# The first and the last stretch of a two-layer hybrid encoder: zeros ahead of the data, squares in place, later tables, a shorter last root, outputs on two queues

## The chip, the core and the metric

The kernel runs on one core of a Trainium2 chip. The metric is the device time of one execution in microseconds. The core's engines work from queues of their own, each in order: TensorE (PE, with its weight loads as PEld), VectorE (DVE), ScalarE (ACT), GpSimd (POOL) and SyncE (SP), which issues the DMAs.

## What is computed

Two layers, each with four sequence mixers behind one input projection, a cross attention and an MLP; a norm at the end. x is 512 rows of 1024, all in float32.

```python
for l in range(DEPTH):
    h = rmsnorm(x, norm_mix[l])
    z = h @ w_in[l]
    (rq, rk, rv, rg, lx, lg, cq, ckv, kr, gqkv, gg, gb, ga) = split_cols(z, IN_SIZES)
    y_a = retention(rq, rk, rv, rg, positions, ret_gn[l])
    y_b = rg_lru_branch(lx, lg, ...)
    y_c = mla(cq, ckv, kr, positions, ...)
    y_d = gated_deltanet(gqkv, gg, gb, ga, ...)
    x = x + jnp.concatenate([y_a, y_b, y_c, y_d], axis=-1) @ w_out[l]
    x = x + memory_xattn(rmsnorm(x, norm_xattn[l]), rmsnorm(mem, norm_mem[l]), ...)
    h = rmsnorm(x, norm_mlp[l])
    x = x + jnp.square(jax.nn.relu(h @ mlp_w1[l])) @ mlp_w2[l]
return rmsnorm(x, final_norm)
```

rmsnorm divides each row by the root of its mean square; retention and mla turn their queries and keys by tables of cosines and sines of the positions (the tables).

## The kernel before

x lies in SBUF with its 1024 features on the partitions: eight tiles `xr[k]` of 128x512. A float32 product is made of three matmuls at a reduced-precision type: both operands are split into a high part (an ACT copy, `xh`, `wh`) and a low part (a DVE subtraction, `xl`, `wl`), and hi x hi, lo x hi and hi x lo are summed in PSUM (`mm3_cm`, L287). A plain f32 matmul is recorded as two instructions.

**Weights** come in units of 128x1024 (some of 128x720), in the order of `PLAN`. `wload` (L262) issues one unit's DMA on SP, splits it on ACT and DVE; there are two raw buffers, three of `wh`, two of `wl`. `wnext` (L279) keeps two units loaded ahead.

**Order of the work.** The program is traced in Python order, and a planner orders each engine's queue ahead of time by priority and by when it reckons an instruction to be ready. `lane(key, base)` (L201) gives the instructions traced in it a priority: within a layer the weights (w) come first, then evacuations (ev, 1.5), LRU (1.7), gated DeltaNet (gdn, 2), MLA (3), retention (4) and the projections themselves (proj, 6). What is traced outside a lane, at the start of the program, comes ahead of all of these. On the chip each queue runs in that fixed order.

**The start.** L408 to L419 issue the DMAs of the parameters and of x, with the first three weight units among them, the constants and the positions. `norm_tile` (L372) then scales and splits each x tile and squares it on ACT (`square_acc`, L364): the first square is the accumulator `acc` (`xg[2]`), the others go through one buffer `sq` and are added by POOL, the last by DVE. `rope_tables` (L424), called at L1393 ahead of the layers, makes `cosT` and `sinT` with some 26 DVE instructions on 128x128 in one chain and two sines on ACT.

**The gdn projection.** In `layer` (L466), `rstd_of(acc)` (L383) sums the squares over partitions with the ones product (`acc` x `ones`, four f32 matmuls), takes the mean and its inverse root with `rsqrt` (L336: an integer guess and three Newton steps, 12 DVE instructions). It is traced in the gdn lane ahead of `proj_g("gdn", ...)` (L512), whose four units of 24 matmuls write four PSUM banks (two pj, two ch). `bcast` (L393) spreads the inverse root by four matmuls against the identity and an ACT copy. Then six blocks each go through `evz` (a product with the broadcast, L516), a causal convolution (`conv_in`, L521: one ACT and three DVE instructions), tanh, and the gate product `s2[i]` on DVE (L544), beside the projections that follow. The LRU's constants (L914 to L923) are a softplus on 128x2 and a few more tiny DVE steps in the LRU lane, and the DMA of its weights.

**The end.** `last_tile` (L1211) works the last block of the MLP's second product in two halves of 256 columns: a half's products (`prod`), their evacuation and squares (`evac`), the root by `rstd_of(accs[g], 2)`, and `finish(g)`: the broadcast, eight products of 128x256 with it (five on DVE, three on POOL) and eight output DMAs, all issued by SP (L1242).

Of the kernel before, what the change touches and what calls it, by code (L numbers as in the profile page):

```python
# [165 lines left out]
def build(tc, A, out, dbg=None):  # L166
# [63 lines left out]
    def act(o, i, f, **k):  # L230
        ACT.activation(o, i, f, **k)  # L231
# [30 lines left out]
    def wload():  # L262
        u = wstate["loaded"]
        if u >= total:
            return
        wstate["loaded"] += 1
        l, i = divmod(u, len(PLAN))
        n = PLAN[i][1]
        off = l * LAYER_ELEMS + UOFF[i]
        with using("w"):  # L270
            raw = wp.tile([128, n], F32, tag="wraw", name=nm("wr"), bufs=2)
            SP.dma_start(out=raw, in_=A["wu"][off:off + 128 * n].rearrange("(p n) -> p n", p=128))
            hi = wp.tile([128, n], F32R, tag="whi", name=nm("wh"), bufs=3)
            act(hi, raw, AF.Copy)
            lo = wp.tile([128, n], F32R, tag="wlo", name=nm("wl"), bufs=2)
            tt(V, lo, raw, hi.bitcast(F32), SU)
        wstate["tiles"][u] = (hi, lo)

    def wnext(name):  # L279
# [40 lines left out]
    def proj_t(name, xh, xl, n, kper, outs, share=1, ks=None, edge=(True, True)):  # L320
# [12 lines left out]
                        mm(o, xl[k][:, s], wh[:, c], False, edge[1] and k == e1 and t % share == share - 1)  # L333
        return outs

    def rsqrt(o, v, n):  # L336
        t = tiny.tile([128, n], I32, tag=f"rt{n}", name=nm("rt"))
        w = tiny.tile([128, n], F32, tag=f"rw{n}", name=nm("rw"))
        nv = tiny.tile([128, n], F32, tag=f"rn{n}", name=nm("rn"))
        ts(V, t, v.bitcast(I32), 1, ALU.logical_shift_right)  # L340
        ts(V, o.bitcast(I32), t, -1.0, MU, float(0x5f3759df), AD)
        ts(V, nv, v, -0.5, MU)
        for _ in range(3):
            tt(V, w, o, o, MU)
            tt(V, w, w, nv, MU)
            stt(o, w, 1.5, o, AD, MU)
# [33 lines left out]
        acc = xp.tile([128, S], F32, tag="acc", name=nm("acc"))  # L380
        return xh, xl, acc

    def rstd_of(acc, ntt=TT):  # L383
        ps = sct()
        for t in range(ntt):
            mm(ps[:, t:t + 1], acc[:, t * 128:(t + 1) * 128], ones, True, True)
        v = tiny.tile([128, ntt], F32, tag=f"rv{ntt}", name=nm("rv"))
        ts(V, v, ps[:, 0:ntt], 1.0 / D, MU, EPS, AD)
        r = tiny.tile([128, ntt], F32, tag=f"rstd{ntt}", name=nm("rstd"))
        rsqrt(r, v, ntt)  # L390
        return r

    def bcast(r, n=S, pool=None, keep=False):  # L393
# [20 lines left out]
    for l in range(1, NL):  # L414
        SP.dma_start(out=par[l], in_=A["par"][l])
    xg = new_xg()
    for k in range(KT):
        norm_tile(xr[k], P(0, "nmix", k), xg[0][k], xg[1][k], xg[2], k)
    SP.dma_start(out=posi, in_=A["pos"])  # L419

    cosT = cp.tile([128, TT, 32], F32, name="cosT")
    sinT = cp.tile([128, TT, 32], F32, name="sinT")
# [43 lines left out]
    def layer(l):  # L466
# [38 lines left out]
            a, b = pjt(), pjt()  # L505
            return [p[:, i * n:(i + 1) * n] for p in (a, b) for i in range(2)]

        with lane(*GDN):
            rstd = rstd_of(acc)
            rstdh = o16("rstdh", 4)  # L510
            ts(V, rstdh, rstd, 0.5, MU)
        pg = proj_g("gdn", xh, xl, [pjt, pjt, cht, cht])  # L512
        with lane(*GDN):
            rbc = bcast(rstd)

# [20 lines left out]
        for i in range(6):  # L536
            ps = pg[i] if i < 4 else proj_m("gdn", i - 4, xh, xl, new=pjt)
            with lane(*GDN):
                ca = g2()
                zq.append(evz(ps, xtmp(i)))  # L540
                conv_in(zq[i], "gcw", i * 4, ca)
                th = g2()
                act(th, ca, AF.Tanh, scale=0.5)
                stt(s2[i], th, 1.0, ca, AD, MU)  # L544
                if i < 4:
                    act(zq[i], s2[i], AF.Square)
        with lane(*GDN):
            for i in range(4):
                for t in range(TT):
                    mm(ssq[:, t * 8 + 2 * i:t * 8 + 2 * i + 2], zq[i][:, t * 128:(t + 1) * 128], C("hsel"), True, True)  # L550
# [360 lines left out]
        with lane(*MLA):  # L911
            mla()

        with lane(*LRU):  # L914
            spl, sp2, spn, sp4 = o16("spl", 2), o16("sp2", 2), o16("spn", 2), o16("bah", 4)
            ts(V, spl, P(l, "lam", 0, 2), -1.0, MU)
            softplus(sp2, spl, 2)
            ts(V, spn, sp2, -4.0, MU)
            ts(V, sp2, sp2, 2.0, MU)
            ts(V, sp4[:, 0:2], P(l, "lba", 0, 2), 0.5, MU)  # L920
            ts(V, sp4[:, 2:4], P(l, "lbx", 0, 2), 0.5, MU)
            wl_ = op.tile([128, 4, 128], F32, tag="wlru", name=nm("wlru"))
            SP.dma_start(out=wl_, in_=A["wlru"][l])  # L923
# [287 lines left out]
        def last_tile(facc, hh, hl, r2):  # L1211
# [22 lines left out]
            def finish(g):  # L1234
                s = slice(g * 256, g * 256 + 256)
                b, bp = bcast(rs[g], 256, mp, True)
                for m in range(8):
                    if m in (2, 5, 7):
                        tt(G, xr[m][:, s], xr[m][:, s], b, MU)
                    else:  # L1240
                        tt(V, xr[m][:, s], xr[m][:, s], bp, MU)
                    SP.dma_start(out=out[:, m, s], in_=xr[m][:, s])  # L1242

            prod(0, range(16))
            evac(0)
            prod(1, range(8))
            rs[0] = rstd_of(accs[0], 2)
            prod(1, range(8, 16))
            evac(1)
            finish(0)  # L1250
            rs[1] = rstd_of(accs[1], 2)
            finish(1)

        pv = [[bank("lg"), cht()], []]
# [135 lines left out]
            xg = nx  # L1390
        stk.close()

    rope_tables()  # L1393
    for l in range(NL):
        layer(l)
    ctx.close()
# [79 lines left out]
```

## Time and profile before

| | us |
|---|---|
| median of the runs | 1670.68 |
| the runs | 1667.58, 1674.56, 1670.68 |
| span of the profiled execution, first to last instruction | 1662.2 |
| TensorE busy | 1629.5 |
| VectorE busy | 909.0 |
| ScalarE busy | 679.0 |
| GpSimd busy | 105.9 |

The profile is that of one execution; the page gives its span and no other time of it. Times in the rows are microseconds from the span's start. An engine counts as busy from the start of an instruction to its modelled end, so matmuls that follow one another overlap, and their spacing is read from the starts. PEclk is the TensorE clock that was granted, as a share of 2.4 GHz.

### The profile page before, as it was taken

What the parts mean: (1) busy time and instruction counts of PE and PEld (TensorE: products, weight loads), DVE (VectorE), ACT (ScalarE), POOL (GpSimd) and SP (SyncE); (2) the same over time, 40 slices, a digit from 0 to 9 for tenths busy, and PEclk for the clock granted to TensorE, in tenths of its full rate; (3) what the DMA queues carried; (4) which work ended last, traced back from release to release, by engine and by line L of the source; (5) the groups of instructions that cost most, each with busy time, mean ns of one, the idle gap of its engine ahead of it and who ended that gap; (6) DMA issues with size and microseconds to landing.
All of it is one profiled execution on the core that took longest, in us unless ns stands there. A gap on an engine that the chain in (4) does not pass through costs nothing.

```text
span 1662.2 us, 23657 instructions
## 1 busy us (share of the span) xinstructions
PE 1629.5 (98%) x9408; PEld 1343.6 (81%) x9408; DVE 909.0 (55%) x1989; ACT 679.0 (41%) x1169; POOL 105.9 (6%) x96
## 2 busy tenths in 40 slices
PE   6999999999999999999999999999999999999997
PEld 5868789888888888888886787998888888888886
DVE  6886578455555422443368855774563643234433
ACT  5565454344443312432235545543453432124331
POOL 2000000110010010000101000002001000100011
PEclk8999999999999999999999999999999999999998
DMA  4211023332122222223331111253312222222222
GB/s 169 84 39 52 27 92 124 138 122 81 51 90 97 93 97 94 101 90 120 114 103 58 52 40 38 87 168 133 106 52 76 93 98 99 92 99 92 101 89 77
DMA packets 47919, 150.69 MB, mean 91 GB/s; under 512 B 5696, under 2 KB 9792, under 8 KB 47808
## 3 DMA queue, kind: packets, MB, share of 16 engines
q1 hardware_dynamic: 47808, 149.17, 26.3%
q8 instruction: 74, 1.21, 0.3%
q14 instruction: 37, 0.30, 0.1%
HBM read 144.96 MB, written 4.19 MB: 90 GB/s over the span
## 4 chain that ended last, share of the span: by engine, by line
PE 90%; DVE 5%; DMA 2%; ACT 1%; issue 1%; POOL 0%; SPq 0%; POOLq 0%; ACTq 0%; DVEq 0%
PE pj L234 28%; PE ch L234 28%; PE gd L234 23%; PE lg L234 8%; DMA wr<-in_wu 2%; PE ch L402 2%; DVE wl L219 1%; ACT wh L231 1%; DMA mem<-in_memT 1%; DVE g L649 1%; DVE bf L228 0%; DVE sp L222 0%; DVE xl L222 0%; POOL x L219 0%; DVE kv L219 0%
## 5 line engine op out<-in xcount | busy, mean ns | idle before, releaser
L219 DVE TENSOR_TENSOR wl<-wr,wh 128x1024 fp32r<-128x1024 f32 (+1 forms) x256 | 311.3, 1216 | 553.3 <-PE pj L234 181.0
L231 ACT ACTIVATE wh<-wr 128x1024 fp32r<-128x1024 f32 (+1 forms) x256 | 269.6, 1053 | 622.1 <-PE pj L234 204.6
L234 PE MATMUL pj<-xh,wh 128*128 128x512 f32 x288 | 115.6, 402 | 6.8 <-ACT wh L231 6.8
L234 PE MATMUL pj<-xl,wh 128*128 128x512 f32 x288 | 115.6, 401 | 0.0
L234 PE MATMUL pj<-xh,wl 128*128 128x512 f32 x288 | 114.8, 399 | 0.0
L219 POOL TENSOR_TENSOR acc<-acc,sq 128x512 f32<-128x512 f32 x42 | 64.6, 1537 | 762.4 <-ACT sq L231 762.4
L234 PE MATMUL pj<-wh,xl 128*128 128x256 f32 (+1 forms) x352 | 107.5, 306 | 0.0
L234 PE MATMUL ch<-xh,wh 128*128 128x512 f32 x272 | 106.9, 393 | 0.0
L234 PE MATMUL ch<-xl,wh 128*128 128x512 f32 x272 | 106.6, 392 | 0.0
L234 PE MATMUL ch<-xh,wl 128*128 128x512 f32 x272 | 106.4, 391 | 0.0
L234 PE MATMUL pj<-wh,xh 128*128 128x256 f32 (+1 forms) x352 | 106.3, 302 | 0.0
L234 PE MATMUL pj<-wl,xh 128*128 128x256 f32 (+1 forms) x352 | 105.3, 299 | 0.0
L234 PE MATMUL ch<-hh,wh 128*128 128x512 f32 x192 | 75.8, 395 | 0.0
L234 PE MATMUL ch<-hl,wh 128*128 128x512 f32 x192 | 75.8, 395 | 0.0
L234 PE MATMUL ch<-hh,wl 128*128 128x512 f32 x192 | 75.8, 395 | 0.0
L234 PEld LDWEIGHTS pj<-wh,xl 128*128 128x128 f32 x352 | 68.5, 194 | 4.0 <-issue 1.8
L234 PEld LDWEIGHTS pj<-wh,xh 128*128 128x128 f32 x352 | 68.3, 194 | 3.2 <-issue 0.9
L234 PEld LDWEIGHTS pj<-xh,wh 128*128 128x128 f32 x288 | 55.0, 191 | 19.3 <-ACT wh L231 6.8
L234 PEld LDWEIGHTS pj<-wl,xh 128*128 128x128 f32 x352 | 68.4, 194 | 2.4 <-issue 0.8
L219 DVE TENSOR_TENSOR hl<-s,hh 128x512 fp32r<-128x512 f32 x64 | 44.2, 691 | 39.2 <-ACT hh L231 39.0
L234 PEld LDWEIGHTS pj<-xl,wh 128*128 128x128 f32 x288 | 54.8, 190 | 13.2 <-issue 2.3
L234 PEld LDWEIGHTS pj<-xh,wl 128*128 128x128 f32 x288 | 54.7, 190 | 12.6 <-issue 0.9
(533 smaller groups left out, 3791.0 us busy)
## 6 DMA issues: line engine op xcount, KB each, us to landing
wr<-in_wu SPq DMA_DIRECT2D x248, 512.0 KB, 3.5
x<-in_xT SPq DMA_DIRECT2D x16, 256.0 KB, 3.7
wr<-in_wu SPq DMA_DIRECT2D x8, 360.0 KB, 2.8
mem<-in_memT SPq DMA_DIRECT2D x16, 128.0 KB, 3.4
xs<-x SPq DMA_DIRECT2D x8, 256.0 KB, 2.6
x<-xs SPq DMA_DIRECT2D x8, 256.0 KB, 3.2
out<-x SPq DMA_DIRECT2D x16, 128.0 KB, 1.8
big<-in_wmla SPq DMA_DIRECT2D x2, 640.0 KB, 5.9
```

The costliest lines, as they stand in the source:

```text
L219: e.tensor_tensor(o, a, b, op=op)
L231: ACT.activation(o, i, f, **k)
L234: PE.matmul(o, lhsT=l, rhs=r, start=st, stop=sp, **k)
L402: PE.transpose(o, i, ident)
L649: V.transpose(Nt3[32 * q:32 * q + 32].rearrange("m j i -> m i j"), src)
```

## The change

Ten places, all in the first stretch and the last, but for the LRU constants, which are moved in both layers.

- `wload`: the first unit is loaded and split in two column halves, each with its own DMA, ACT copy and DVE subtraction.
- The start: `acc` is first set to zero on DVE, and three f32 matmuls on it (512, 512 and 256 columns) are issued on TensorE into the bank lg. The x tiles are scaled and split without the squares.
- `first_acc`: the squares are made later, on ACT, in place over the x tiles (the first into `acc`), and added by DVE. It is traced ahead of the gdn projection's third unit, in the proj lane (layer 0).
- `norm_in`: the ones product and the root are traced ahead of the fourth unit in the proj lane (layer 0), or as before ahead of the first in the gdn lane (layer 1).
- `rope_tables` is traced behind the fourth gate product, outside any lane; `tc.issue_after(after.ins)` puts those of its instructions that run on DVE behind that product in DVE's queue (an order of issue, no wait). The LRU constants' DVE instructions get the same bound, in both layers.
- `rsqrt1` takes the place of `rsqrt` in `last_tile`: a root on ACT, a reciprocal and one Newton step on DVE.
- The outputs of odd m are issued by ACT, the others by SP.

```diff
@@ -269,11 +269,15 @@
         off = l * LAYER_ELEMS + UOFF[i]
         with using("w"):
             raw = wp.tile([128, n], F32, tag="wraw", name=nm("wr"), bufs=2)
-            SP.dma_start(out=raw, in_=A["wu"][off:off + 128 * n].rearrange("(p n) -> p n", p=128))
+            src = A["wu"][off:off + 128 * n].rearrange("(p n) -> p n", p=128)
             hi = wp.tile([128, n], F32R, tag="whi", name=nm("wh"), bufs=3)
-            act(hi, raw, AF.Copy)
             lo = wp.tile([128, n], F32R, tag="wlo", name=nm("wl"), bufs=2)
-            tt(V, lo, raw, hi.bitcast(F32), SU)
+            cuts = [slice(0, n // 2), slice(n // 2, n)] if u == 0 else [slice(0, n)]
+            for c in cuts:
+                SP.dma_start(out=raw[:, c], in_=src[:, c])
+            for c in cuts:
+                act(hi[:, c], raw[:, c], AF.Copy)
+                tt(V, lo[:, c], raw[:, c], hi[:, c].bitcast(F32), SU)
         wstate["tiles"][u] = (hi, lo)
 
     def wnext(name):
@@ -333,6 +337,16 @@
                         mm(o, xl[k][:, s], wh[:, c], False, edge[1] and k == e1 and t % share == share - 1)
         return outs
 
+    def rsqrt1(o, v, n):
+        w = tiny.tile([128, n], F32, tag=f"rw{n}", name=nm("rw"))
+        nv = tiny.tile([128, n], F32, tag=f"rn{n}", name=nm("rn"))
+        act(o, v, AF.Sqrt)
+        ts(V, nv, v, -0.5, MU)
+        V.reciprocal(o, o)
+        tt(V, w, o, o, MU)
+        tt(V, w, w, nv, MU)
+        stt(o, w, 1.5, o, AD, MU)
+
     def rsqrt(o, v, n):
         t = tiny.tile([128, n], I32, tag=f"rt{n}", name=nm("rt"))
         w = tiny.tile([128, n], F32, tag=f"rw{n}", name=nm("rw"))
@@ -380,14 +394,14 @@
         acc = xp.tile([128, S], F32, tag="acc", name=nm("acc"))
         return xh, xl, acc
 
-    def rstd_of(acc, ntt=TT):
+    def rstd_of(acc, ntt=TT, root=rsqrt):
         ps = sct()
         for t in range(ntt):
             mm(ps[:, t:t + 1], acc[:, t * 128:(t + 1) * 128], ones, True, True)
         v = tiny.tile([128, ntt], F32, tag=f"rv{ntt}", name=nm("rv"))
         ts(V, v, ps[:, 0:ntt], 1.0 / D, MU, EPS, AD)
         r = tiny.tile([128, ntt], F32, tag=f"rstd{ntt}", name=nm("rstd"))
-        rsqrt(r, v, ntt)
+        root(r, v, ntt)
         return r
 
     def bcast(r, n=S, pool=None, keep=False):
@@ -414,9 +428,22 @@
     for l in range(1, NL):
         SP.dma_start(out=par[l], in_=A["par"][l])
     xg = new_xg()
+    warm = xg[2]
+    V.memset(warm, 0.0)
+    wps = bank("lg")
+    for n in (512, 512, 256):
+        mm(wps[:, 0:n], warm[:, 0:128], warm[:, 0:n], True, True)
     for k in range(KT):
-        norm_tile(xr[k], P(0, "nmix", k), xg[0][k], xg[1][k], xg[2], k)
+        gc = P(0, "nmix", k)
+        act(xg[0][k], xr[k], AF.Copy, scale=gc)
+        stt(xg[1][k], xr[k], gc, xg[0][k].bitcast(F32), MU, SU)
     SP.dma_start(out=posi, in_=A["pos"])
+
+    def first_acc():
+        for k in range(KT):
+            act(xr[k] if k else xg[2], xr[k], AF.Square)
+            if k:
+                tt(V, xg[2], xg[2], xr[k], AD)
 
     cosT = cp.tile([128, TT, 32], F32, name="cosT")
     sinT = cp.tile([128, TT, 32], F32, name="sinT")
@@ -505,11 +532,20 @@
             a, b = pjt(), pjt()
             return [p[:, i * n:(i + 1) * n] for p in (a, b) for i in range(2)]
 
-        with lane(*GDN):
-            rstd = rstd_of(acc)
-            rstdh = o16("rstdh", 4)
-            ts(V, rstdh, rstd, 0.5, MU)
-        pg = proj_g("gdn", xh, xl, [pjt, pjt, cht, cht])
+        rs_ = {}
+
+        def norm_in(u):
+            if l == 0 and u == 2:
+                with using("proj"):
+                    first_acc()
+            if u == (3 if l == 0 else 0):
+                with (using("proj") if l == 0 else lane(*GDN)):
+                    rs_["r"] = rstd_of(acc)
+                    rs_["h"] = o16("rstdh", 4)
+                    ts(V, rs_["h"], rs_["r"], 0.5, MU)
+
+        pg = proj_g("gdn", xh, xl, [pjt, pjt, cht, cht], pre=norm_in)
+        rstd, rstdh = rs_["r"], rs_["h"]
         with lane(*GDN):
             rbc = bcast(rstd)
 
@@ -541,9 +577,14 @@
                 conv_in(zq[i], "gcw", i * 4, ca)
                 th = g2()
                 act(th, ca, AF.Tanh, scale=0.5)
-                stt(s2[i], th, 1.0, ca, AD, MU)
+                last = V.scalar_tensor_tensor(s2[i], th, 1.0, ca, op0=AD, op1=MU)
                 if i < 4:
                     act(zq[i], s2[i], AF.Square)
+            if i == 3:
+                after = last
+                if l == 0:
+                    with tc.issue_after(after.ins):
+                        rope_tables()
         with lane(*GDN):
             for i in range(4):
                 for t in range(TT):
@@ -911,7 +952,7 @@
         with lane(*MLA):
             mla()
 
-        with lane(*LRU):
+        with lane(*LRU), tc.issue_after(after.ins):
             spl, sp2, spn, sp4 = o16("spl", 2), o16("sp2", 2), o16("spn", 2), o16("bah", 4)
             ts(V, spl, P(l, "lam", 0, 2), -1.0, MU)
             softplus(sp2, spl, 2)
@@ -1239,16 +1280,16 @@
                         tt(G, xr[m][:, s], xr[m][:, s], b, MU)
                     else:
                         tt(V, xr[m][:, s], xr[m][:, s], bp, MU)
-                    SP.dma_start(out=out[:, m, s], in_=xr[m][:, s])
+                    (ACT if m % 2 else SP).dma_start(out=out[:, m, s], in_=xr[m][:, s])
 
             prod(0, range(16))
             evac(0)
             prod(1, range(8))
-            rs[0] = rstd_of(accs[0], 2)
+            rs[0] = rstd_of(accs[0], 2, rsqrt1)
             prod(1, range(8, 16))
             evac(1)
             finish(0)
-            rs[1] = rstd_of(accs[1], 2)
+            rs[1] = rstd_of(accs[1], 2, rsqrt1)
             finish(1)
 
         pv = [[bank("lg"), cht()], []]
@@ -1390,7 +1431,6 @@
             xg = nx
         stk.close()
 
-    rope_tables()
     for l in range(NL):
         layer(l)
     ctx.close()
```

## Rows read from the trace of the kernel before

**Rows 1.** The page, part 1: busy time and share of each engine.

```profile
PE 1629.5 (98%) x9408; PEld 1343.6 (81%) x9408; DVE 909.0 (55%) x1989; ACT 679.0 (41%) x1169; POOL 105.9 (6%) x96
```

**Rows 2.** Waits of PE over the whole span: us in total, times, longest.

```profile
PE pj L234 <- ACT wh L231: 6.8, 1, 6.8
...
PE gd L234 <- DVE acc L219: 6.4, 1, 6.4
...
PE gd L402 <- DVE kv L219: 1.0, 1, 1.0
```

**Rows 3.** Timeline, end of the span: start, us, engine, line, op.

```profile
1650.97 0.15 DVE L228 TENSOR_SCALAR rv<-gd 128x2 f32<-128x2 f32 x1
...
1653.16 0.16 DVE L222 SCALAR_TENSOR_TENSOR rstd<-rw,rstd 128x2 f32<-128x2 f32 x1
...
1653.46 1.20 PE L234 MATMUL gd<-cst,rstd 128*128 128x128 f32 x4 [2.75 <-DVE rstd L222]
...
1655.97 3.76 SPq L1242 DMA_DIRECT2D out<-x  x8
```

**Rows 4.** Busy time by stretch, columns first; layer 0, then layer 1.

```profile
core 0: us, PE busy (x) PEld busy (x) DVE busy (x) ACT busy (x) POOL busy (x), PEclk, DMA share, GB/s
6.84:42.54 35.70, 29.26 (x113) 23.40 (x113) 28.52 (x75) 18.39 (x27) 9.55 (x6) 0.86 0.44 159
42.54:326.65 284.11, 281.65 (x2298) 232.53 (x2297) 203.31 (x584) 143.78 (x306) 8.36 (x12) 0.99 0.24 79
...
830.15:854.34 24.19, 24.11 (x114) 19.65 (x112) 13.99 (x47) 7.16 (x11) 0.00 (x0) 1.00 0.36 129
854.34:1143.73 289.39, 285.13 (x2298) 235.37 (x2297) 205.37 (x584) 144.73 (x306) 8.50 (x12) 0.98 0.24 78
```

**Rows 5.** Timeline of PE, first 43 us.

```profile
9.97 0.63 PE L234 MATMUL pj<-xh,wh 128*128 128x512 f32 x1
...
10.40 0.63 PE L234 MATMUL pj<-xl,wh 128*128 128x512 f32 x1
...
25.35 1.86 PE L234 MATMUL gd<-cst,acc 128*128 128x1 f32 x8 [6.40 <-DVE acc L219]
...
37.09 0.40 PE L234 MATMUL pj<-xh,wh 128*128 128x512 f32 x1
```

**Rows 6.** Groups of instructions, first 61 us: busy, mean ns | idle.

```profile
L219 POOL TENSOR_TENSOR acc<-acc,sq 128x512 f32<-128x512 f32 x6 | 9.5, 1591 | 11.5 <-ACT sq L231 11.5
```

**Rows 7.** Timeline of all engines, first 45 us.

```profile
2.81 0.20 ACT L231 ACTIVATE sp<-spl 128x2 f32<-128x2 f32 x1 [0.79 <-DVE spl L226]
...
5.14 0.61 ACT L231 ACTIVATE acc<-x 128x512 f32<-128x512 f32 x1
...
5.73 1.06 ACT L231 ACTIVATE wh<-wr 128x1024 fp32r<-128x1024 f32 x1
...
6.95 0.72 ACT L231 ACTIVATE xh<-x,par 128x512 fp32r<-128x512 f32 x1 [0.16 <-DMA x<-in_xT]
...
8.44 0.91 SPq L410 DMA_DIRECT2D x<-in_xT  x2
...
30.67 1.28 ACT L231 ACT_TABLE_LOAD   x1
```

**Rows 8.** Timeline of DVE, 20 to 63 us.

```profile
23.70 0.16 DVE L428 CAST pf<-posi 128x4 f32<-128x4 int32 x1
...
38.43 0.22 DVE L228 TENSOR_SCALAR cosT<-rn__186 128x128 f32<-128x128 f32 x1
...
61.88 0.69 DVE L222 SCALAR_TENSOR_TENSOR g<-g,g 128x512 f32<-128x512 f32 x1 [0.62 <-ACT g L231]
```

**Rows 9.** Timeline of PE, 80 to 84 us.

```profile
82.23 1.98 PE L234 MATMUL gd<-g,cst 128*128 128x512 f32 x4
```

**Rows 10.** DMA, first 16 us (us to landing), then rates of 1655.9 to 1661.2.

```profile
x<-in_xT SPq DMA_DIRECT2D x8, 256.0 KB, 5.9
...
GB/s 0 0 0 0 0 0 54 309 340 248 170 340 325 186 232 363 302 132 278 340 278 124 348 317 240 193 340 348 132 255 356 302 124 309 356 255 23 0 0 0
```

## The prediction, made before the change was run

> **What bounds the kernel now.** I read the busy shares first. TensorE is busy for 1629.5 of 1662.2 us [rows 1], so there are 32.7 us of idle time in the whole span, and only what lies in idle time or at the low clock can be won. The waits of TensorE, longest first, say where: 6.8 us before the first matmul and 6.4 us at the ones product that sums the squares [rows 2]; every wait inside the two layers is 1.0 us or less. The rest of the large idle time lies at the end, where the last matmuls, those of a broadcast, start only at 1653.46 [rows 3].
>
> The third view cuts layer 0 and layer 1 at the same points of their work: from the first matmul of the gdn projection to the first matmul of its next part (96 matmuls of 128x512, the ones product, the broadcast), and from there to the last product of w_out with the same tile [rows 4]. Layer 0 takes 35.70 and 284.11 us, layer 1 takes 24.19 and 289.39 us. The same work costs layer 0 11.5 us more at its start: that is what the change can win there. But the rest costs layer 1 5.3 us more: it idles for 4.3 us against 2.5, and its mean clock is 0.98 against 0.99. A layer that starts without a stall gave part of it back.
>
> In the front itself [rows 5] the matmuls begin at 6.84, are 0.43 us apart (9.97 to 10.40; 512 columns at 1.2 GHz), and 0.227 us apart later (24 of them from 37.09 to 42.54, the cut of [rows 4]: 2.4 GHz). The ones product starts at 25.35 after 6.40 us of idle time. The granted clock of the stretch is 0.86 [rows 4], since it fell to half in that idle time. Stretches before 11.3 us show a clock of 1.00 although the matmuls are 0.43 us apart, so there I go by the spacing.
>
> Why the ones product is late is read on ACT and POOL. POOL adds six squares at 1.59 us each and waits 11.5 us for them [rows 6]. ACT's next square has one buffer and so waits for POOL, and the splits of x and of the weights queue behind it on ACT.
>
> **The change, part by part.** Times are on the profiled execution's clock.
>
> *First matmul.* The square that ran from 5.14 to 5.73 goes [rows 7]. The weight split follows at 5.14 on half the columns; 0.61 us (the square's duration for 512 columns) instead of 1.06. With the 0.05 us hand-over of now (5.73 + 1.06 to 6.84) the first matmul starts at 5.80; I take 5.85. This needs the first half of the weights by 5.14; all of them were there by 5.73, so the bounds are 5.80 and 6.40. The extra DMA on SP costs SP one issue, beside transfers that are still under way.
>
> *Matmuls on zeros.* They wait for a memset of 512 columns on DVE, between 0 and the 0.69 us of a step of two inputs of that size [rows 8]: ready by about 1.5. Two f32 matmuls of 512 columns, recorded as four instructions, take 1.98 us at full clock [rows 9], so 0.43 each with the drain of the last one taken off; the zeros (512, 512 and 256 columns) are worth five of them, at half clock 4.3 us, done by 5.8. So they end just as the first true matmul may start: cost 0, and at most 0.3. What they should buy is the full clock from the first true matmul.
>
> *Unit 0.* The second x tile lands at 6.95 [rows 7]; its split takes ACT and DVE some 0.7 each, until 8.4, and with two more matmuls the seventh may start at 8.85 (now 9.97). So six matmuls spread over 3.0 us where 1.36 would do: 1.64 us that stay lost. The rest of the front at full clock is what layer 1 takes: 5.85 + 1.64 + 24.19 = 31.7, against 42.54. That is 10.8 us. If the clock were half until 11.25 as now, five or six matmuls cost 0.2 us more each: 1.1 us less won.
>
> *Squares in place, ones product later.* ACT's squares (eight, 0.61 each) leave the front of its queue, POOL's six adds leave POOL, and DVE gets six more, 0.69 each as its other steps of two inputs and 512 columns [rows 8]. Each in-place square now also waits until DVE has split its x tile. ACT can't split the last x tile before it lands: issued by 9.35 [rows 7], 5.9 us to landing [rows 10], so near 15.3 and, with its split, 16.0. The eight squares and one weight split after it are at most 5.9 us more, about 21.9; the last add follows at 22.6. The ones product now stands after three units: 5.85 + 1.64 + 72 x 0.227 = 23.8. So it is covered by 1.2 us. If the cover is gone, TensorE waits again; bounds 0 to 2.5 us, I take 0.5. Behind it on TensorE stands unit 3. What is late next is the broadcast, which needs the root; its steps are no longer mixed with the tables on DVE, and unit 3 (5.45 us) covers it.
>
> *Tables and LRU constants.* On DVE the tables run from 23.70 to 38.65, 15 us with other work between [rows 8]; the LRU constants are 20 tiny steps at 0.16 [rows 3], 3.2 us. Both go behind the fourth gdn gate product (now at 61.88 [rows 8], then some ten us sooner). The issue order is bound on DVE only: the LRU weights' DMA on SP isn't moved, and nothing new waits on SP. The two sine activations on ACT follow by their data, with two table loads as now (1.28 each [rows 7]). What queues behind them are the last two gdn convolutions and the weight splits of the moment. DVE and ACT aren't the bound there while TensorE has projections to do, so I cost it at nothing by itself and put it into the term below. In layer 1 the constants move too: 3.2 us on DVE, 0 for the time, bounds plus and minus 1.
>
> *Given back in the mixer.* Between 0 (layer 0's rest as it is) and 5.3 us (layer 1's rest) [rows 4]. Layer 1 is the nearer row for a start without a stall, yet about 3 us of the 5.3 are clock (2% of 289 less 1% of 284), and nothing in these rows ties that to the start. I take the middle, 2.6.
>
> *Last root.* Now 12 DVE steps after the sum: from 1650.97 to 1653.32 [rows 3]. Then: the sum's step, one ACT root (0.20, [rows 7]), four DVE steps at 0.20 apart, two hand-overs: 1.2 us, so 1.1 are saved. The root's table load lies in ACT's idle time. But ACT now issues outputs too, and the root may stand behind one or two of them at 0.48 each: I take off 0.4 and count 0.7, bounds 0.1 and 1.1. The broadcast after it takes 1.20 at half clock, and may come before the clock falls: 0 to 0.6, I take 0.3.
>
> *Outputs by two queues.* Eight issues run from 1655.97 for 3.76 us [rows 3], 0.48 apart. Halved, that would save 1.9 us. But the row of rates [rows 10] shows 340 to 363 GB/s in its best slices: 131 kB in 0.37 us, so the transfers themselves allow only 7 x 0.11 = 0.8, and some tenths more for an earlier first issue. I take 1.0, bounds 0.5 and 1.9. The Trainium skill, "DMA: Bandwidth & Descriptors", section "Issuing engines are not separate DMA queues", speaks against more: several issuing engines share the same transfer engines and save only issue time. By that rule alone the term is 0.8; by the issue pace alone it would be 1.9.
>
> **Sum.** Front 10.8 - 0.5, mixer -2.6, end 0.7 + 0.3 + 1.0: 9.7 us. The span would go from 1662.2 to 1652.5. The median of the runs is 1670.68, 8.5 us above this span, with runs from 1667.58 to 1674.56; the same 9.7 us off it gives 1661.0.
>
> **The rivals.**
> A, the forecast: TensorE stays the bound and at most 4 us come back. For it: waits of TensorE inside the layers are tiny in both layers [rows 2, 4]. With none given back 1658.4; with 4 given back, 1662.4.
> B, all of layer 1's loss appears, or a little more, since the tables add to DVE in a stretch where it is already busy: 10.3 - 5.3 + 2.0 = 7.0 us, 1663.7. For it: layer 1 itself. Against: most of the loss is clock.
> C, the change doesn't do what it says: the squares come late, because ACT does them last and each waits for DVE, and TensorE waits at the ones product as before, at half clock after it. 6 of the 10.8 us go: 1667.0.
> D, slower: the tables set the time. If the gdn chain on DVE, not TensorE, decides the end of the mixer, then 15 + 3.2 us of steps and 2.6 us of table loads stand in it after the fourth gate product, and the chain starts only the front's 10.3 us sooner: 10.5 us late, less 2.0 at the end: 1679.2. It decides from the point at which TensorE runs out of projections. Against it: TensorE's idle time from 42.54 on is 2.5 us in 284 [rows 4].
>
> **How the numbers follow.** A 0.60, B 0.26, C 0.10, D 0.04. The time is A's, 1661.0. A measurement of this kernel can tell about 0.5%, 8.4 us, from no change: faster means below 1662.3. That is A; B and C are within; D is slower: 0.60, 0.36, 0.04. The range of 8 in 10 reaches from A's best case (10.8 at the front, nothing given back, 3.6 at the end: 1656.3, less 2 for the runs' spread) to C: 1654.5 to 1667.5.
>
> **What would show it.** First true matmul near 5.9 and matmuls 0.227 apart from about 9; no TensorE wait at the ones product, now behind 72 matmuls; the first matmul of the next part near 32; the same last product of w_out in layer 0 near 319, not 326.65; root to broadcast 1 us shorter; eight last outputs in about 3 us on two queues. It is wrong if TensorE shows new waits of over 2 us between 40 and 330 (for weight splits held behind the tables on DVE or the sine on ACT), or if the ones product still waits.

## The result, and the profile after

The changed kernel is slower: 1679.91 us in the median (1674.06 to 1686.86) against 1672.15 us of the kernel before beside it, a ratio of 1.0069 [1.0044, 1.0093]. The forecast was 1661.0, faster. The profiled execution of the changed kernel took 1682.89 us, its span is 1681.1 us. Executions of one kernel differ by how long TensorE's clock is at half in each, so the tables below give the span times its mean granted clock (what it would be at full clock) beside the time. The medians leave out the runs more than 1.5% above the fastest of their kernel (one each of e1, e6 and e7, two each of e2 and e8, three of e14, which lost 42 to 67 us to the clock); the profiles of e7 and e14 are of such runs and are read for the order of the work and its waits.

The span splits at the same points of the work as [rows 4], in us:

| stretch | before | after | forecast |
|---|---|---|---|
| start to the first matmul of the next part | 42.54 | 31.46 | 32.2 |
| from there to the same last product of w_out | 284.11 | 314.90 | 286.7 |
| to the ones product of the last half (at 1650.11, 1669.91) | 1323.46 | 1323.55 | as before |
| from there to the end | 12.09 | 11.19 | 10.1 |

The front gave 11.1 us (10.3 forecast); the end gave 0.9 of 2.0; all the rest is one number, 30.8 us lost in the mixer of layer 0 between these two profiles. Busy time by stretch of the kernel after, for the first two lines (us; busy time and count of each engine; PEclk is the granted clock as a share of 2.4 GHz):

```profile
core 0: us, PE busy (x) PEld busy (x) DVE busy (x) ACT busy (x) POOL busy (x), PEclk, DMA share, GB/s
5.84:31.46 25.62, 24.71 (x114) 19.61 (x113) 18.91 (x38) 15.74 (x23) 0.00 (x0) 1.00 0.67 232
31.46:346.36 314.90, 311.55 (x2298) 256.16 (x2297) 210.42 (x634) 147.67 (x313) 8.00 (x12) 0.88 0.22 72
```

The second line has the same 2298 matmuls as [rows 4] and no more idle time than before to speak of (3.4 us against 2.5), but a mean clock of 0.88 against 0.99. TensorE's waits in that stretch of the kernel after (total, times, longest) show that nothing holds it up:

```profile
engine line waited for: us in total, times, longest us
PE lg L234 <- DVE xt L222: 1.0, 1, 1.0
PE ch L416 <- DVE qf L219: 0.8, 1, 0.8
PE gd L234 <- DVE g L717: 0.5, 1, 0.5
PE ch L416 <- ACT o L231: 0.4, 1, 0.4
PE ch L416 <- DVE bf L219: 0.2, 1, 0.2
```

So the place is looked for by the clock, in slices of 20 us. The kernel after, and then the kernel before:

```profile
140.00:160.00 20.00, 20.00 (x256) 17.33 (x251) 4.86 (x16) 4.77 (x14) 0.00 (x0) 0.50 0.08 28
160.00:180.00 20.00, 20.00 (x140) 16.03 (x138) 4.79 (x18) 7.25 (x21) 0.00 (x0) 0.50 0.00 1
180.00:200.00 20.00, 20.00 (x97) 14.19 (x95) 8.07 (x29) 4.76 (x14) 0.00 (x0) 0.50 0.09 27
200.00:220.00 20.00, 20.00 (x118) 15.02 (x118) 7.45 (x29) 5.52 (x15) 0.00 (x0) 0.65 0.01 1
```

```profile
140.00:160.00 20.00, 20.00 (x253) 17.22 (x250) 11.63 (x23) 11.62 (x25) 0.00 (x0) 0.91 0.13 41
160.00:180.00 20.00, 20.00 (x177) 15.55 (x175) 12.30 (x42) 8.06 (x22) 0.00 (x0) 1.00 0.19 66
180.00:200.00 20.00, 20.00 (x173) 15.74 (x173) 11.36 (x42) 9.67 (x28) 0.00 (x0) 1.00 0.08 28
```

TensorE is at 1.2 GHz for 60 us, for 14 of the next 20 (0.65) and for the last one before 140, some 75 us; in the kernel before for 3.6 us. It shows as busy all the time (its last wait before that, 0.5 us, ended at 135.7), and DVE is busy for 4.8 us of 20 where it was for 11.6: nobody waits for DVE. Half of 75 is 37 us (1.8 in the kernel before); 30.8 us more than before show in the stretch.

What TensorE does there is the gated DeltaNet's triangular solve (matmuls of 16 and 32 columns) and then its scan. The groups of matmuls from the solve's first to the scan's first product, in the kernel after (143.3 to 164.7):

```profile
L234 PE MATMUL gd<-g,g 32*32 32x32 f32 x128 | 7.3, 237 | 0.0
L234 PE MATMUL gd<-g,g 16*32 16x16 f32 x128 | 6.4, 210 | 0.0
L234 PE MATMUL pj<-wh,xh 128*128 128x256 f32 x5 | 2.6, 520 | 0.0
L234 PE MATMUL pj<-wl,xh 128*128 128x256 f32 x5 | 2.2, 449 | 0.0
L234 PE MATMUL pj<-wh,xl 128*128 128x256 f32 x5 | 2.1, 415 | 0.0
```

and in the kernel before (136.8 to 157.0):

```profile
L234 PE MATMUL pj<-wh,xl 128*128 128x256 f32 x21 | 6.9, 326 | 0.0
L234 PE MATMUL pj<-wh,xh 128*128 128x256 f32 x21 | 6.6, 314 | 0.0
L234 PE MATMUL pj<-wl,xh 128*128 128x256 f32 x21 | 6.2, 295 | 0.0
L234 PE MATMUL gd<-g,g 32*32 32x32 f32 x128 | 4.8, 192 | 0.0
L234 PE MATMUL gd<-g,g 16*32 16x16 f32 x128 | 3.9, 178 | 0.0
```

The small matmuls are the same; beside them stood 63 wide ones of the projections and now 15. Ahead of the solve the trace counts 489 wide matmuls instead of 368: TensorE came early, the solve came late (143.3 instead of 136.8), and the projections were used up in between. That is what I set out to test; a count beside a clock is no cause yet.

### The profile page after: what moved, and what is told of

Its sections match the earlier page's. It is cut to its first block, busy times and chain, and to the rows that moved or that the text cites. A ratio compares the mean times of both kernels' runs of the same rounds, so it can differ in the third digit from the quotient of the medians.

```text
span 1681.1 us, 23666 instructions
## 1 busy us (share of the span) xinstructions
PE 1659.6 (99%) x9414; PEld 1364.0 (81%) x9414; DVE 905.7 (54%) x1983; ACT 680.8 (40%) x1173; POOL 96.5 (6%) x90
## 4 chain that ended last, share of the span: by engine, by line
PE 90%; DVE 6%; DMA 2%; ACT 1%; issue 1%; POOL 0%; SPq 0%; POOLq 0%; ACTq 0%; DVEq 0%
PE ch L234 28%; PE pj L234 28%; PE gd L234 23%; PE lg L234 8%; PE ch L416 2%; DMA wr<-in_wu 1%; DVE wl L219 1%; DMA x<-in_xT 1%; DVE xt L222 1%; DVE g L690 1%; ACT wh L231 0%; DVE g L716 0%; DVE rm L219 0%; DVE xt L219 0%; DVE g L219 0%
## 5 line engine op out<-in xcount | busy, mean ns | idle before, releaser
L219 DVE TENSOR_TENSOR wl<-wr,wh 128x1024 fp32r<-128x1024 f32 (+2 forms) x257 | 311.7, 1213 | 540.6 <-PE pj L234 170.7
L231 ACT ACTIVATE wh<-wr 128x1024 fp32r<-128x1024 f32 (+2 forms) x257 | 269.9, 1050 | 617.7 <-PE ch L234 185.5
L234 PE MATMUL pj<-wh,xh 128*128 128x256 f32 (+1 forms) x352 | 110.8, 315 | 0.0
L234 PE MATMUL pj<-wl,xh 128*128 128x256 f32 (+1 forms) x352 | 109.6, 311 | 0.0
L219 POOL TENSOR_TENSOR acc<-acc,sq 128x512 f32<-128x512 f32 x36 | 55.0, 1527 | 752.6 <-ACT sq L231 752.6
```

Source lines behind the costliest of these rows:

```text
L219: e.tensor_tensor(o, a, b, op=op)
L234: PE.matmul(o, lhsT=l, rhs=r, start=st, stop=sp, **k)
```

## The experiments

Each row is one kernel. "Wide" is the number of projection matmuls between the solve's first matmul and the scan's first product, in its trace (by their starts; the groups above take in one more, which runs over the edge); "at full clock" is span times mean clock, "lost" the rest of the span, medians in us.

| kernel | tables | bound in layer | wide | at full clock | lost (range) | ratio to before |
|---|---|---|---|---|---|---|
| before (95 runs) | start | none | 62 | 1646.0 | 21.7 (12 to 32) | 1 |
| changed, first runs | later | 0, 1 | 14 | 1638.8 | 40.3 (33 to 47) | 1.0069 |
| e10 changed, again | later | 0, 1 | 14 | 1637.5 | 51.5 (35 to 52) | 1.0102 [1.0058, 1.0146] |
| e9 | later | 0 | 14 | 1638.2 | 38.6 (28 to 59) | 1.0074 [1.0044, 1.0105] |
| e2 | later | none | 25 | 1642.4 | 19.1 (15 to 23) | 0.9950 [0.9932, 0.9968] |
| e1 | start | 0, 1 | 52 | 1645.1 | 26.7 (10 to 37) | 1.0005 [0.9972, 1.0037] |
| e12 | start | 0 | 52 | 1644.1 | 20.8 (15 to 37) | 1.0005 [0.9975, 1.0036] |
| e7 | start | 1 | 46 | 1643.6 | 12.4 (10 to 13) | 0.9923 [0.9900, 0.9947] |
| e3 | start | none | 46 | 1641.0 | 16.6 (10 to 23) | 0.9934 [0.9909, 0.9959] |
| e14 | start | none | 11 | 1643.3 | 42.1 (22 to 51) | 1.0090 [1.0055, 1.0125] |
| e4 the moves in the kernel before | later | 0, 1 | 21 | 1646.6 | 27.7 (17 to 40) | 1.0041 [1.0002, 1.0079] |

In the profiles, one run each, half clock around the solve and the scan of layer 0 lasts 3.4 us before, 7 in e1 and e3, 14 in e4, 17 in e2, 20 in e12, and 48, 51 and 75 in e9, e10 and the changed kernel's first. The three kernels with 14 wide matmuls have the long stretches; above that the count doesn't rank the kernels (e1, with 52, loses more than e2, with 25).

**Which part of the change.** Four kernels undo or do the two moves (tables behind the fourth gate product; the LRU constants' bound); e1 to e3 keep all the rest of the change. e3 undoes both:

```diff
-                if l == 0:
-                    with tc.issue_after(after.ins):
-                        rope_tables()
...
-        with lane(*LRU), tc.issue_after(after.ins):
+        with lane(*LRU):
...
+    rope_tables()
     for l in range(NL):
```

e1 undoes the first alone, e2 the second alone, and e4 makes both in the kernel before.

> The changed kernel with the tables traced at the start again, ahead of the layers; the LRU constants keep their bound. Theory T (the tables, 16.8 us of DVE time from 54.97 on, hold up the gdn chain while TensorE works off its projections; the triangular solve and the scan then find few projections beside them, and the granted clock stays at half): little half clock between 120 and 230 us (under 25 us of it, 75 in the changed kernel), scan's first product before 155 us (164.7), median 1655 to 1666. Rival F (the shorter front alone does it, since TensorE comes ahead of the gdn chain): half clock for 60 us or more as in the changed kernel, median 1675 to 1687. Rival L (the bound on the LRU constants does it): as F.

> The changed kernel without the bound on the LRU constants; the tables stay behind the fourth gate product. T: 60 us or more at half clock in layer 0, median 1675 to 1687. L: under 25 us at half clock, median 1655 to 1666. F: as T.

> The changed kernel with both moves undone (tables at the start, LRU constants free): the new front and the new end alone. T and L: under 25 us at half clock in layer 0, front won (next part's first matmul near 32), median 1655 to 1664. F: 60 us or more at half clock, 1675 to 1687.

> The kernel before with only the two moves (tables and LRU constants behind the fourth gate product). T: next part's first matmul still near 42 us, then 50 us or more at half clock around the triangular solve and the scan; median 1685 to 1700, slower than the kernel before by 0.8% or more. F: no more half clock than the kernel before, 1665 to 1676. Rival D (the chain on DVE itself sets the end of the mixer): slower too, but with TensorE waiting for DVE for over 5 us in the scan.

e3 took 1660.11 us: without the moves the change does what was forecast (1661.0). Its front ends at 31.96, and from there to the ones product ahead of the cross attention it takes 341.74 us, where the kernel before takes 338.81 and the changed one 369.59. First e3, then the changed kernel, then the kernel before (timeline of TensorE; start, duration):

```profile
31.96 0.42 PE L234 MATMUL ch<-wh,xh 128*128 128x360 f32 x1
373.70 0.83 PE L234 MATMUL gd<-cst,acc 128*128 128x1 f32 x7
```

```profile
31.46 0.39 PE L234 MATMUL pj<-xh,wh 128*128 128x512 f32 x1
401.05 0.83 PE L234 MATMUL gd<-cst,acc 128*128 128x1 f32 x7
```

```profile
381.35 0.72 PE L234 MATMUL gd<-cst,acc 128*128 128x1 f32 x6
```

So the shorter front (F) is not the cause by itself: in e3 it gives back 2.9 us (in a profile of 1654.55 us, one of e3's fastest). But T, the tables alone, isn't either: e2 has them moved, 17 us at half clock in its profile, and took 1663.29 us where T said 1675 to 1687 (two more of its ten runs, at 1695.03 and 1698.21, lost 56 and 61 us to the clock, so the tables alone can draw a long stretch now and then). Nor L, the bound alone, though e2 fits it: for e1, which keeps the bound, L said 60 us or more at half clock and 1675 to 1687; its profile has 7 us there, and it took 1672.51, outside L's range and T's. e4 was slower than the kernel before as T said, by less (1.0041 [1.0002, 1.0079], 1676.68 us; 27.7 us lost against 21.7), with no wait of TensorE for DVE over 1.0 us between the front and the end, so D fell there. It takes both moves for the whole loss.

**Layer 0 or layer 1.** The bound stands in both layers. e7, e9 and e12 keep it in one:

```diff
-        with lane(*LRU), tc.issue_after(after.ins):
+        with lane(*LRU), (ExitStack() if l else tc.issue_after(after.ins)):
```

(e9 with the tables moved, e12 with the tables at the start; e7 the other way round.) e10 is the changed kernel once more.

> As e3, but the LRU constants keep their bound in layer 1 (layer 0 is that of e3, layer 1 that of the changed kernel). If what e1 lost against e3 (median 1673 against 1660) is lost in layer 1: median 1668 to 1678, widely spread, mean clock 0.984. If in layer 0: as e3, 1657 to 1664, mean clock 0.99.

> The changed kernel with the LRU constants' bound kept in layer 0 only (layer 1 is that of the kernel before, layer 0 that of the changed kernel). If the time is lost in layer 0, by the two moves together: over 28 us lost to the clock (span less span times mean clock) in nearly every run, 45 us or more at half clock around the solve and the scan, median 1671 to 1682. If it was layer 1 in most runs: lost under 22, median 1655 to 1664.

> The changed kernel once more, beside the others, to see how often the long stretch at half clock comes: as in its first six runs (lost 33 to 47 us, median 1680); layer 0 at half clock for over 45 us in the profile. If those six were chance: lost near 20 as in e2, median near 1662.

> As e3, but the LRU constants keep their bound in layer 0 only (tables at the start, layer 1 as in the kernel before). It fills the fourth place of the square: tables moved or not, constants bound or not, layer 1 left alone. If the constants' bound alone brings long half clock into layer 0: lost 25 us or more, median over 1668. If it takes both moves (between the 128 small matmuls of the solve and the scan's first product the order has 5.9 us of projections here, 5.2 in e3, 2.8 in e2, 1.6 in e9): as e3, lost 13 to 20, median 1656 to 1664.

e9 loses what the changed kernel loses, with layer 1 as it was: layer 0 is enough for the loss. e10 lost more than the first runs did (1689.44 us, 51 us at half clock in layer 0). e7 loses nothing against e3 in four of its five runs. e12 lies between: 1667.87 us, neither case's range, 4 us more lost than e3 and 3 more at full clock. Against e3's 1660.11 us the moved tables cost 3.2 (e2), the bound in layer 0 costs 7.8 (e12), and both together cost 18.6 (e9). In e9 the clock has the shape of the changed kernel's, only shorter:

```profile
140.00:160.00 20.00, 20.00 (x263) 17.50 (x259) 4.85 (x17) 6.70 (x20) 0.00 (x0) 0.56 0.09 28
160.00:180.00 20.00, 20.00 (x126) 14.62 (x126) 5.30 (x21) 5.08 (x15) 0.00 (x0) 0.50 0.00 1
180.00:200.00 20.00, 20.00 (x129) 15.48 (x129) 9.81 (x35) 6.46 (x20) 0.00 (x0) 0.74 0.08 27
```

e10's profile has such a stretch in layer 1 too, beside that of layer 0:

```profile
960.00:1010.00 50.00, 50.00 (x388) 41.70 (x386) 18.78 (x41) 20.02 (x40) 0.00 (x0) 0.56 0.08 25
```

44 us at half clock there, 6.8 in the changed kernel's first profile. The longest run of e7 (1682.61 us), the one profiled, has 44 us in layer 1 too. Both have the bound in layer 1; what decides there from run to run is not settled.

**The order alone.** e14 takes e3, moves nothing, and adds one order of issue on TensorE: the solve's first small matmul behind the 57th of the retention's query projection, which e3 has beside the solve.

```diff
+            tc.add_manual_dep(mms[solve[0]].ins, mms[n0 + 56].ins.name,
+                              mybir.DependencyInfo(mybir.DependencyClass.NoSync, mybir.DependencyReason.DATA), reason="late solve")
```

> As e3 (no table and no constant moved), with one order of issue added on TensorE in layer 0: the first small matmul of the solve stands behind the 57th matmul of the retention's query projection. So 87.1 us of projections stand ahead of the solve (80.3 in e3, 87.1 in e9) and 1.2 us between it and the scan's first product (5.2 in e3, 1.6 in e9); DVE's and ACT's work is that of e3. Theory O (the place of the projections in TensorE's order makes the long half clock, whatever DVE does): 40 us or more at half clock in layer 0 in the profile, lost 28 to 45 us, median 1670 to 1685. If the moves act in another way (DVE's tables, the LRU's steps): as e3, lost 13 to 23, median 1658 to 1666.

1685.85 us in the runs compared (1690.46 over all), ratio 1.0090 [1.0055, 1.0125]; 42.1 us lost against e3's 16.6, and at full clock only 2.3 us more. The tables and the constants stand where e3 has them. (The median is 0.9 us above theory O's range, and the profile is that of the longest run.) So neither move is needed: a new order in layer 0 with the projections ahead of the solve is enough to make the loss. What in this order does it is not shown. The edit moves the solve later as well (154.5 instead of 135.1), the planner orders DVE's and ACT's queues anew from about 130 us on (with the same instructions), and TensorE has a wait until 134.2 that neither e3 nor the changed kernel has (total, times, longest):

```profile
PE ch L236 <- ACT o L231: 3.5, 1, 3.5
```

The clock fell around that wait and was back at full before the long stretch began, at 152.5, beside the solve.

**Wide matmuls added.** e6 is the changed kernel, e13 is e9, each with 68 matmuls of 128x512 that nobody reads, in layer 0: 15.4 us of added work at full clock (68 x 0.227).

```diff
+        def fill(ps, n):
+            if l == 0:
+                for _ in range(n):
+                    mm(ps, xh[0][:, 0:128], xh[0], True, True)
             ps = sct()
+            fill(ps, 8)
```

(8 ahead of each of three groups of the solve, 2 behind each `sct()` of the scan.)

> The changed kernel with 70 extra matmuls of 128x512 in layer 0 (24 ahead of the three groups of small matmuls of the triangular solve, 46 in the scan, into PSUM that the true ones overwrite): 16 us of work at full clock that nobody reads. Theory T2 (the granted clock falls and stays at half because too few wide matmuls stand beside the small ones): span times mean clock rises from 1638.8 to some 1654, but the time lost to the clock falls from 40 to under 22 us; under 25 us at half clock in layer 0; median 1670 to 1678, in spite of the extra work. Rival (half clock has another cause, such as a long time of high load before it): lost stays at 35 or more, median 1690 to 1702.

> As e9 (both moves, layer 0 only), with the 68 extra matmuls of e6 in layer 0 (24 in the solve, 44 in the scan, 15.4 us at full clock). e6's three slow runs had layer 1's bound, this one hasn't. T2 (sparse wide matmuls let the clock fall and keep it low): lost 10 to 20 us in nearly every run against 38.6 in e9, span times mean clock near 1654, median 1664 to 1672, below e9's 1678.7 in spite of the added work. If half clock isn't set by what stands beside the small matmuls: lost as in e9, median 1690 or more.

e6: 15 us more work and yet 1668.94 us against the changed kernel's 1679.91; at full clock 1655.0 us, as counted, lost 11.7 instead of 40.3 (three of its ten runs lost 30, 34 and 49). e13: at full clock 1652.4, lost 25.2 instead of 38.6, 1678.88 us, as long as e9. The direction is the expected one in both, the size only in e6. Their layer 0 has the same order on TensorE, DVE and ACT, yet the profiles differ, so part of this is the spread from run to run. First e6, then e13:

```profile
140.00:160.00 20.00, 20.00 (x244) 16.20 (x242) 6.74 (x24) 8.07 (x22) 0.00 (x0) 0.89 0.01 3
160.00:180.00 20.00, 20.00 (x167) 13.64 (x165) 10.77 (x40) 10.37 (x30) 0.00 (x0) 1.00 0.08 28
```

```profile
140.00:160.00 20.00, 20.00 (x176) 16.54 (x175) 3.71 (x11) 6.16 (x16) 0.00 (x0) 0.50 0.01 3
160.00:180.00 20.00, 20.00 (x134) 13.23 (x134) 9.03 (x33) 6.93 (x21) 0.00 (x0) 0.76 0.08 27
```

One reason for the missing effect is in the trace: 16 of the 24 matmuls meant for the solve ran at 95 to 98 us, since their bank was free then, and only 10 of the added ones fell between the solve and the scan. The planner also moved the rest (the solve starts at 135.8). So this supports the theory only weakly.

**LRU behind gdn.** With the tables moved, the planner starts the LRU's gate products at 83.27 us (110.2 before), ahead of the solve's DVE work. e8 is the changed kernel with the LRU's lane behind the gdn lane in layer 0:

```diff
-        EV, GDN, MLA, RET, LRU = LN("ev", 1.5), LN("gdn", 2), LN("mla", 3), LN("ret", 4), LN("lru", 1.7)
+        EV, GDN, MLA, RET, LRU = LN("ev", 1.5), LN("gdn", 2), LN("mla", 3), LN("ret", 4), LN("lru", 2.5 if l == 0 else 1.7)
```

> The changed kernel with the LRU's lane behind the gdn lane in layer 0 (2.5 instead of 1.7), both moves kept. Theory S (with the tables moved, the planner puts the LRU's steps, first gate product at 83 instead of 110 us, ahead of the gdn chain on DVE and the solve comes late): solve's 128 small matmuls by 136 us (143 in the changed kernel), scan's first product by 155 (165), 18.5 us of projections in the scan instead of 15; half clock under 30 us, median 1655 to 1668. If only the projections between the solve and the scan count (1.8 us of them here, 1.6 in the changed kernel, 5.2 in e3): half clock for 50 us or more, median 1672 to 1687.

The solve's 128 small matmuls start at 131.8, the scan's first product at 150.4; 27 us at half clock, 21.7 lost, 1666.71 us, ratio 0.9994 [0.9972, 1.0016]; two more of its ten runs lost 49 and 54. Theory S's numbers held. Beside the solve there are but 16 wide matmuls (14 in the changed kernel), so their count there isn't the whole measure: the scan has 163 here and 132 there (137 in e3). Together with e14 this run shows that the order decides: here both moves stay and most of the loss goes, there neither is made and the loss comes.

**The end and the zeros.** e5 is e3 with the first half's outputs all on SP; e11 is e3 without the matmuls on zeros.

```diff
-                    (ACT if m % 2 else SP).dma_start(out=out[:, m, s], in_=xr[m][:, s])
+                    (ACT if g and m % 2 else SP).dma_start(out=out[:, m, s], in_=xr[m][:, s])
```

> As e3 (tables at the start, LRU constants free), and the first half's outputs are all issued by SP, so that ACT's last root stands behind no output; the second half's outputs keep both queues. Expected: from the mean's step (rv) to the root's last step 1.3 us instead of 2.1 in the changed kernel and 2.35 in the kernel before; layer 0 and 1 as in e3; median 1656 to 1663. If the root wasn't held up by the issues, 2.1 us as before.

> As e3, without the matmuls on zeros. The working of the prediction: without them the clock is half until some 11 us, matmuls 0.43 us apart; next part's first matmul 1.1 us later than in e3 (33.1 instead of 32.0), median 1 us above e3's, 1658 to 1665. If the zeros do more (a longer half clock in the front): next part's first matmul at 34 or later.

The last root in the kernel after, and then in e5:

```profile
1669.56 2.30 ACTq L1283 DMA_DIRECT2D out<-x  x4
1670.77 0.15 DVE L228 TENSOR_SCALAR rv<-gd 128x2 f32<-128x2 f32 x1
1671.90 0.20 ACT L231 ACTIVATE rstd<-rv 128x2 f32<-128x2 f32 x1 [2.12 <-DVE rn L226]
1672.73 0.16 DVE L222 SCALAR_TENSOR_TENSOR rstd<-rw,rstd 128x2 f32<-128x2 f32 x1
1673.04 1.20 PE L234 MATMUL gd<-cst,rstd 128*128 128x128 f32 x4 [2.52 <-DVE rstd L222]
```

```profile
1647.62 0.15 DVE L228 TENSOR_SCALAR rv<-gd 128x2 f32<-128x2 f32 x1
1647.80 0.20 ACT L231 ACTIVATE rstd<-rv 128x2 f32<-128x2 f32 x1 [1.17 <-DVE rv L228]
1648.63 0.16 DVE L222 SCALAR_TENSOR_TENSOR rstd<-rw,rstd 128x2 f32<-128x2 f32 x1
1648.93 1.20 PE L234 MATMUL gd<-cst,rstd 128*128 128x128 f32 x4 [1.57 <-DVE rstd L222]
```

In the kernel after ACT issues four outputs until 1671.86, and only then makes the root whose input was there at 1670.92. From the mean's step to the end of the root: 2.35 us before [rows 3], 2.12 after, 1.17 in e5. The time of e5 (1661.25, ratio 0.9946 [0.9919, 0.9973]) can't be told from e3's.

Without the zeros the first matmuls are 0.79 and 0.59 us apart until 10.19 and 0.43 from there (e11, then the kernel after):

```profile
6.41 0.79 PE L234 MATMUL pj<-xh,wh 128*128 128x512 f32 x1 [6.41 <-ACT xh L231]
7.20 0.79 PE L234 MATMUL pj<-xl,wh 128*128 128x512 f32 x1
10.19 0.63 PE L234 MATMUL pj<-xh,wh 128*128 128x512 f32 x1
35.21 0.43 PE L234 MATMUL ch<-wh,xh 128*128 128x360 f32 x1 [0.70 <-ACT wh L231]
```

```profile
5.84 0.74 PE L234 MATMUL pj<-xh,wh 128*128 128x512 f32 x2
7.36 0.39 PE L234 MATMUL ch<-xh,wh 128*128 128x512 f32 x1
7.58 0.39 PE L234 MATMUL ch<-xl,wh 128*128 128x512 f32 x1
24.14 0.95 PE L234 MATMUL gd<-cst,acc 128*128 128x1 f32 x8
```

The next part starts at 35.21 instead of 31.96: 3.3 us, not 1.1, of which 0.70 is a wait for a weight split. The median (1659.89, ratio 0.9935 [0.9915, 0.9956]) doesn't show them; the profile of e3 waits 1.92 us for DVE at 34.30, soon after its earlier start, where e11 waits 0.78.

## Why the prediction was wrong

**The step that failed is "Given back in the mixer".** It was put between 0 and 5.3 us, from the two layers of [rows 4], and taken as 2.6; it measured 30.8 in the two profiles (by the medians, 18.6 us more are lost to the clock). Both rows came from one order of TensorE's queue, and I took them as the ends for a change that makes the planner order the mixer anew. Without the two moves e3 gives back 2.9 us and lands on the forecast; with both the order is another one, and no row of before bounded that. The clock stood in the step only as 3 us of the difference between two rows, and not as a price of its own: [rows 4] had a clock of 0.98 to 0.99, so a stretch at half was not looked for.

**"Tables and LRU constants ... I cost it at nothing by itself".** Right for DVE: it had room (4.8 us busy of 20), and the tables ran from 54.97 to 71.73, 16.8 us for the 15 forecast. The wrong part is that the step asked only who waits for DVE. Nobody did for long; the moves brought the solve later (143.3 instead of 135.1 in e3) and changed what TensorE had left when it came.

**Rival D gave 1679.2, and 1679.9 was measured.** That agreement is chance. It has the gdn chain 10.5 us late and that time added at the end of the mixer; the solve did come late, by 6.5 us (143.3 instead of 136.8), but no wait of TensorE over 1.0 us was added for it. Its point, "from which TensorE runs out of projections", was the right one: TensorE ran out, went on with small matmuls, and paid by the clock and not by waiting.

**"It is wrong if TensorE shows new waits of over 2 us between 40 and 330".** There were none over 1.0, so this sign would not have shown a loss of 30 us. The granted clock of the stretch should have been named there.

**The front was right, step by step.** First true matmul 5.84 (5.85), the first on the second x tile at 8.87 (8.85; it was the ninth and not the seventh), the ones product at 24.14 behind 72 matmuls (23.8) without a wait, next part at 31.46 (31.7, and 32.2 with the 0.5 us of waiting that the sum counts). The zeros' share was too small: 1.1 counted, 3.3 measured (e11, with the wait of 0.70), as without them the first matmuls are up to 0.79 apart, and half clock lasts until 14.0 us, where I had taken half clock to last until 11.25 as in the kernel before. Rival C's late squares didn't come: the last add ended at 22.16 (22.6).

**The end was sized too large: 0.9 of 2.0 us.** The root saved 0.2 (0.7 taken, 0.1 as the lower bound), since it stood behind four issues of ACT and not "one or two". Freed of them it saves 1.2 (e5). The broadcast saved nothing (1.20 us as before; 0.3 taken). From the broadcast to the end it is 8.06 us against 8.74: 0.7 for the outputs (1.0 taken). The Trainium skill, "DMA: Bandwidth & Descriptors", section "Issuing engines are not separate DMA queues", let me put 0.8 by its rule alone; the trace agrees with it, at 0.7.

**The rest of the account.** At full clock the changed kernel is 7.2 us shorter than the kernel before (1638.8 against 1646.0), and it loses 18.6 us more to the clock (40.3 against 21.7). Together that is 11 us slower by these medians, 8 beside the runs of its own session.

The version that beats both is e3: the new front and end without either move, 0.9934 [0.9909, 0.9959].

## What to carry to other kernels

Ask of every change to a planned or listed order what order TensorE has around its small matmuls afterwards: here an early TensorE had worked off the projections before the solve came, and it paid at half clock without one long wait. Read the granted clock of each stretch beside busy time and waits, and multiply span by mean clock before two times are compared. When several moves come in one change, run the change without each before the moves are blamed or kept; here the two that were meant to cost nothing cost it all, and most of it only together.

## What the runs showed of the hardware

TensorE stayed at 1.2 GHz for some 75 us while the trace shows it busy throughout and no wait of it in that stretch (139 to 214); its last one before it took 0.5 us, at 135.7. The Trainium skill, "TensorE: Matmul & The Clock Gate", section "HAM oscillation — how this bites in real kernels", lays the fall of the clock to gaps in which TensorE idles for data; this trace differs: the clock fell after a wait of 0.5 us and stayed down through a stream of small matmuls with no gap.

Within one kernel the clock explains the spread: the changed kernel's first six runs lie between 1674.06 and 1686.86 us, 12.8 us apart, while span times mean clock lies between 1635.7 and 1639.9. The same program draws a longer or a shorter stretch at half clock from run to run (lost 33 to 47 us), so one profile of it is one draw.
